# RG-LRU stage in a written TensorE order with its own PSUM, and the later adaLN sums moved to other stages

## The chip, the cores and the metric

The kernel runs on one core of a Trainium2 chip. The metric is device time in microseconds. The core's engines are PE (TensorE), DVE (VectorE), ACT (ScalarE), POOL (GpSimd) and SP (SyncE, which here only issues DMAs); each takes its own instructions in the order in which they stand.

## The reference, cut to what matters

One layer: adaLN modulation, a token mixer with two branches (a bidirectional RG-LRU and a latent attention), their merge, and a mixture of experts. 1024 latent tokens, 256 context tokens, width 1024. What the change touches:

```python
mod = silu(c) @ w_ada + b_ada          # six rows of 1024: shift, scale, gate, twice
z   = modulate(rmsnorm(x)) @ w_in      # RG-LRU input, gelu gate, q/kv latents, sigmoid gates
def rglru_coeffs(x, w_a, b_a, w_x, b_x, lam):
    r = jax.nn.sigmoid(block_diag_linear(x, w_a, b_a))
    i = jax.nn.sigmoid(block_diag_linear(x, w_x, b_x))
    log_a = -RG_C * r * jax.nn.softplus(-lam)
    a = jnp.exp(log_a)
    return a, jnp.sqrt(-jnp.expm1(2.0 * log_a)) * (i * x)
# h = scan(a, b) in both directions over a width-4 convolution of z; y_rnn = (gelu(z') * h) @ w_rnn_out
```

The first two rows of `mod` (shift and scale of the first norm) are needed before anything else. The other four, called m = 0 to 3 in the kernel, are needed from the merge of the branches on.

## The kernel before, in words

Every large matmul is made in three passes (lines 97 to 99, `mm3`): an operand is split by `split` into a high part (an ACT cast, line 93, names ending in h) and the rest (a DVE subtract, line 94, names ending in l), and high×high, high×low and low×high are summed in PSUM. Weights stream from memory through `fetch`: 512 KB into `wr`, split into `wh` and `wl` of three buffers each. A list `items` says in which order; `nextw` takes the next and fetches `LOOK` items ahead.

Where nothing else is said, a scheduler sets the order of instructions on each engine; `tc.manual_schedule` keeps the named engines in the order of the code. Four stages follow one another around the change.

1. q/k/v stage: `qkv` for each of ten token tiles, with blocks of the gelu and sigmoid gates in between (`fill_block`). TensorE's `tp`, `kv`, `zq` and `z` belong to it.
2. RG-LRU stage: eight blocks b of 128 channels. `conv_part(b+1)` projects (48 matmuls `z0` of 512 columns, 24 `z0c` of 256 for the context) and convolves with one ACT and three DVE operations (`xr`, lines 589 and 592). `lru_part(b)` makes four gates (two directions, r and i), each six matmuls `gz` of 512 columns and three `gc` of 256, read by two ACT sigmoids (lines 610 and 611), then tanh, exp, sqrt and DVE scans. `sig_block` makes a sigmoid block `zg` (48 matmuls of 512 columns) of the merge gates; there are 12 in the stage, one to three behind each block b by `sig_plan`. The PSUM comes from two helpers: `pa` (three buffers of two banks: z0, gz, zg, mp) and `pb` (two buffers of one bank: z0c, gc). ACT alone is in written order here.
3. RNN output: for each of eight blocks b of output channels, 96 matmuls `ro` (k = 0 to 7, two halves, three passes) over `rh`/`rl`, the split rows of the RG-LRU's result, then on DVE `s<-ro` (line 821): ro times the sigmoid block, loaded from memory and stored back. Head 0's attention is prepared meanwhile (`qkt`, `pm`, DVE row maxima `mx`, `kl`, `ql`).
4. Attention itself (`s`, and so on).

The adaLN rows m are made by 32 calls of `mod_step`, eight (k) for each m: a 512 KB load of `w_ada` on SP's queue, and on DVE `acc += w_ada[k] * c[k]` (line 395, `acc` 128×1024, one buffer). The eighth call sums `acc` over partitions on TensorE (`mp`, a matmul with ones, line 401), copies the row out on ACT (line 402) and stores it to `mod_d`. A new m begins with a POOL memset of `acc`. All 32 calls stand behind the first eight sigmoid blocks of stage 2, four behind each:

```python
sig_block((s0_d, s1_d)[w][bb], rest if n == 0 else load_rn if b == KD - 1 else None)
for _ in range(4):
    if steps:
        mod_step(steps.pop(0))
```

The router's bias `lb` is made from m = 1 and 2 at the head of stage 3 (`mrow2`, `mc`, `lb`, lines 708 to 720).

Of the kernel before, what the change touches and what calls it, by code (L numbers as in the profile page):

```python
# [24 lines left out]
OP = mybir.AluOpType  # L25
# [35 lines left out]
def layer_kernel(ctx: ExitStack, tc: tile.TileContext, I, rope_tab, out, dbg=None):  # L61
# [324 lines left out]
    def mod_step(j):  # L386
        m, k = divmod(j, KD)
# [18 lines left out]
    with pool("p2") as p2:  # L406
# [151 lines left out]
        for j, i in enumerate(order):  # L558
# [3 lines left out]
            for _ in range(MP2):  # L562
                if steps and steps[0] < N2:
                    mod_step(steps.pop(0))


    p3c = pool("p3")
    p3 = p3c.__enter__()
    if True:
        p4c = None  # L570

        def sig_block(dst, mid=None):
            zz = pa("zg")
            zblock(zz)
# [9 lines left out]
        def conv_part(b):  # L584
            zc, zz = pb("z0c"), pa("z0")
# [12 lines left out]
        def lru_part(b, xr, xrh, xrl):  # L598
            gh, gl_ = nextw([2, 2, P])
            gates = []  # L600
            for d in range(2):
                for g, bn in ((0, "ba"), (1, "bx")):
                    gc, gz = pb("gc"), pa("gz")
# [4 lines left out]
                    r = p3.tile([P, TOK], F32, name=("r", "i")[g], bufs=2)  # L608
# [18 lines left out]
            def rest():  # L627
# [33 lines left out]
        with tc.manual_schedule(engines={mybir.EngineType.Activation}):  # L661
# [21 lines left out]
            for b in range(KD):  # L683
# [24 lines left out]
    mrow = p4.tile([16, P], F32, name="mrow2")  # L708
    nc.sync.dma_start(mrow, mod_d[1:3, :].rearrange("m (k p) -> (m k) p", p=P))
    mc_p = pb("mc")  # L710
    nc.tensor.transpose(mc_p[:, 0:16], mrow, ident[0:16, 0:16])
    mc = p4.tile([P, 2, KD], F32, name="mc")
# [99 lines left out]
    for b in range(KD):  # L812
# [454 lines left out]
```

## Time and profile before

| what | value |
|---|---|
| three runs, median (lowest to highest) | 1790.53 us (1787.06 to 1790.93) |
| the profiled execution's own time | 1793.63 us |
| its span in the trace | 1791.9 us |
| mean granted TensorE clock | 0.976 of full |
| q/k/v stage, about 100.0 to 270.2 | 170.2 us, TensorE busy 168.3 |
| RG-LRU stage, 270.2 to 593.9 | 323.7 us, TensorE busy 309.8 |
| RNN output, 593.9 to 695.7 | 101.8 us, TensorE busy 99.6 |

The span is the time from the first to the last recorded instruction; 1.7 us of the run lie around it. Times of rows are from the span's start. A matmul's row gives a modelled length; neighbours overlap, so its cost is the distance to the next start.

### The profile page before, as it was taken

The numbers are of one execution on the slowest core, as the hardware profiler recorded it, in microseconds if no ns is written. First come the engines' busy times: TensorE is split into PE (matmuls) and PEld (weight loads), VectorE is DVE, ScalarE is ACT, GpSimd is POOL, SyncE is SP. The second block draws the span as 40 slices with busy tenths as digits, with TensorE's granted clock in tenths as the row PEclk, the third lists the DMA queues.
The fourth block names the chain that finished last, engine by engine and source line by source line (L and its number), as shares of the span: only waits on it lengthen the run. The fifth ranks groups of instructions, "written<-read, shape, count | busy, mean of one in ns | idle before, by whom it ended". The sixth has DMA issues, their size and how long they took to land.

```text
span 1791.9 us, 21732 instructions
## 1 busy us (share of the span) xinstructions
PE 1687.7 (94%) x7769; PEld 1346.8 (75%) x7769; DVE 1354.7 (76%) x1852; ACT 1029.6 (57%) x1311; POOL 236.3 (13%) x188
## 2 busy tenths in 40 slices
PE   8999999999899999999999899909999999999997
PEld 3788888787677877777677688708888887888875
DVE  4755445898787554787886857578999999999996
ACT  2532325665677313667776533207777777777774
POOL 1123331111121100111110100000100010001000
PEclk8999999999999999999999999959999999999999
DMA  8264444445452854000000457468999999999971
GB/s 324 98 178 105 112 103 115 133 143 178 134 160 94 280 174 161 28 28 28 28 1 0 180 214 254 187 246 311 384 369 395 390 380 379 389 394 371 390 258 24
DMA packets 177291, 363.80 MB, mean 203 GB/s; under 512 B 43264, under 2 KB 93848, under 8 KB 177184
## 3 DMA queue, kind: packets, MB, share of 16 engines
q1 hardware_dynamic: 172576, 345.65, 53.6%
q0 software_dynamic: 4608, 16.78, 4.1%
q8 instruction: 61, 1.00, 0.2%
q14 instruction: 46, 0.38, 0.1%
HBM read 314.84 MB, written 47.54 MB: 202 GB/s over the span
## 4 chain that ended last, share of the span: by engine, by line
PE 67%; DVE 15%; ACT 6%; issue 6%; DMA 3%; POOL 3%; SPq 0%; POOLq 0%; DVEq 0%; ACTq 0%
PE w_e_gate L98 3%; PE w_e_up L98 3%; PE w_e_gate L97 3%; PE w_e_gate L99 3%; PE w_e_down L98 3%; PE w_e_up L99 3%; PE w_e_up L97 3%; PE w_e_down L99 3%; PE w_e_down L97 3%; PE pm L782 2%; PE z L98 2%; PE z L99 2%; POOL st L142 2%; PE z L97 2%; PE xo L97 2%
## 5 line engine op out<-in xcount | busy, mean ns | idle before, releaser
L94 DVE TENSOR_TENSOR wl<-ma,wh 128x1024 fp32r<-128x1024 f32 x198 | 236.1, 1220 | 21.7 <-ACT wh L93 16.4
L93 ACT CAST wh<-ma 128x1024 fp32r<-128x1024 f32 x198 | 206.7, 1053 | 57.1 <-PE w_e_down L99 18.4
L94 DVE TENSOR_TENSOR wl<-me,wh 128x1024 fp32r<-128x1024 f32 x142 | 170.1, 1221 | 21.6 <-ACT wh L93 16.6
L93 ACT CAST wh<-wr 128x1024 fp32r<-128x1024 f32 (+1 forms) x97 | 98.2, 1014 | 138.9 <-PE z L98 54.6
L93 ACT CAST wh<-me 128x1024 fp32r<-128x1024 f32 x142 | 148.5, 1053 | 47.1 <-PE w_e_down L99 15.6
L846 ACT ACTIVATE pr<-s 128x512 f32<-128x512 f32 x160 | 95.6, 599 | 74.1 <-PE s L99 72.7
L784 DVE TENSOR_REDUCE mx<-pm 128x1 f32<-128x320 f32 x256 | 114.3, 483 | 24.6 <-PE pm L782 21.6
L94 DVE TENSOR_TENSOR wl<-wr,wh 128x1024 fp32r<-128x1024 f32 (+1 forms) x97 | 114.0, 1183 | 24.0 <-ACT wh L93 22.4
L98 PE MATMUL z<-xl,wh 128*128 128x512 f32 x320 | 126.1, 394 | 1.7 <-DVE xl L279 1.7
L99 PE MATMUL z<-xh,wl 128*128 128x512 f32 x320 | 125.7, 394 | 0.6 <-POOL wl L325 0.6
L97 PE MATMUL z<-xh,wh 128*128 128x512 f32 x320 | 125.7, 395 | 0.0
L94 DVE TENSOR_TENSOR pl<-pr,ph 128x1024 fp32r<-128x1024 f32 x64 | 81.3, 1270 | 31.8 <-ACT ph L93 25.0
L98 PE MATMUL w_e_up<-wl,xgh 128*128 128x512 f32 x256 | 103.1, 403 | 1.1 <-DVE wl L94 0.9
L98 PE MATMUL w_e_gate<-wl,xgh 128*128 128x512 f32 x256 | 102.7, 401 | 0.0
L97 PE MATMUL w_e_gate<-wh,xgh 128*128 128x512 f32 x256 | 102.5, 400 | 0.0
L98 PE MATMUL w_e_down<-wl,hdh 128*128 128x512 f32 x256 | 101.6, 397 | 0.6
L1213 POOL DMA_INDIRECT out_dram<-y,icol x16 | 36.3, 2267 | 494.7 <-DVE y L1212 494.7
L99 PE MATMUL w_e_down<-wh,hdl 128*128 128x512 f32 x256 | 99.9, 390 | 0.8 <-DVE hdl L94 0.8
L99 PE MATMUL w_e_gate<-wh,xgl 128*128 128x512 f32 x256 | 100.6, 393 | 0.0
L97 PE MATMUL w_e_down<-wh,hdh 128*128 128x512 f32 x256 | 99.9, 390 | 0.2 <-ACT hdh L93 0.2
L97 PE MATMUL w_e_up<-wh,xgh 128*128 128x512 f32 x256 | 100.1, 391 | 0.0
L99 PE MATMUL w_e_up<-wh,xgl 128*128 128x512 f32 x256 | 100.0, 391 | 0.0
(335 smaller groups left out, 4366.5 us busy)
## 6 DMA issues: line engine op xcount, KB each, us to landing
ma<-in_w_e_down_dram SPq DMA_DIRECT2D x68, 512.0 KB, 8.6
ma<-in_w_e_gate_dram SPq DMA_DIRECT2D x66, 512.0 KB, 7.6
ma<-in_w_e_up_dram SPq DMA_DIRECT2D x64, 512.0 KB, 6.4
me<-in_w_e_gate_dram SPq DMA_DIRECT2D x48, 512.0 KB, 6.4
me<-in_w_e_up_dram SPq DMA_DIRECT2D x48, 512.0 KB, 7.1
me<-in_w_e_down_dram SPq DMA_DIRECT2D x46, 512.0 KB, 8.2
wr<-in_w_in_dram SPq DMA_DIRECT2D x32, 512.0 KB, 4.9
wr<-in_w_ada_dram SPq DMA_DIRECT2D x32, 512.0 KB, 3.4
```

The lines of the kernel that those rows point to most:

```text
L93: nc.scalar.copy(h, src)
L94: nc.vector.tensor_tensor(l, src, h.bitcast(F32), OP.subtract)
L97: nc.tensor.matmul(o, lh, rh, start=start, stop=False)
L98: nc.tensor.matmul(o, lh, rl, start=False, stop=False)
L99: nc.tensor.matmul(o, ll, rh, start=False, stop=stop)
L142: nc.gpsimd.tensor_tensor(ap, ap, h, OP.pow)
L782: nc.tensor.matmul(pm[:, 0:320], qh[:, t * P:(t + 1) * P], kh[:, g * 320:(g + 1) * 320], start=True, stop=True)
L784: nc.vector.tensor_reduce(mx[:, g, t:t + 1], pm[:, 0:320], axis=AX.X, op=OP.max)
L846: nc.scalar.activation(pr[:, sl], sp_, AF.Exp)
L1213: nc.gpsimd.indirect_dma_start(out=out_rows, out_offset=bass.IndirectOffsetOnAxis(ap=icol[:, e:e + 1], axis=0), in_=y, in_offset=None, com ...
```

## The change

- The RG-LRU stage gets a PSUM pool of its own: two buffers of two banks shared by z0 and zg (`pz`), one buffer each for gz (two banks), gc and z0c (one bank).
- PE joins ACT in `manual_schedule`. Each of a block's four gates is followed by an eighth (six matmuls) of the block's first sigmoid block (generator `sig_mm`); its other half comes behind the fourth gate. The tanh moves up behind each direction's gates; r gets a third buffer.
- The 32 sums leave the stage. The eight of m = 1 go to the q/k/v stage, one behind each of eight tiles; the other 24 (m = 2, 0, 3) go into the RNN output, four behind each of the blocks b = 0 to 5. The row is written into `acc[0:1]` instead of a tile of its own.
- The RNN output begins with k = 0 to 6 of block 0, k = 0 to 6 of block 1, then k = 7 of both. The last RG-LRU result is stored on GpSimd's queue.
- `mrow2`, `mc`, `lb` move from the head of the RNN output to its end.

```diff
-    steps = list(range(4 * KD))
+    steps = [(m, k) for m in (1, 2, 0, 3) for k in range(KD)]
+    mod_psum = [pa]
...
-            row = mpool().tile([1, D], F32, name="g", tag="sg", bufs=1)
-            mp = pa("mp")
+            row = acc[0:1, :]
+            mp = mod_psum[0]("mp")
...
-            for _ in range(MP2):
-                if steps and steps[0] < N2:
-                    mod_step(steps.pop(0))
+            mod_steps(1, (1,))
+    open_psum("ps3")
+    def pz(name):
+        return ps["p"].tile([P, 1024], F32, name=name, tag="z", bufs=2)
...
+        def sig_mm(look=None):
+            zz = pz("zg")
+            h, l = nextw([KD, P], look)
+            for n in range(2):
+                for k in range(0, KD, 2):
+                    zhalf(zz, h, l, n, (k, k + 1))
+                    yield zz
...
         def lru_part(b, xr, xrh, xrl):
             gh, gl_ = nextw([2, 2, P])
-            gates = []
+            gates, vv = [], []
+            zg = sig_mm(1)
             for d in range(2):
                 for g, bn in ((0, "ba"), (1, "bx")):
-                    gc, gz = pb("gc"), pa("gz")
+                    gc = ps["p"].tile([P, 512], F32, name="gc", bufs=1)
+                    gz = ps["p"].tile([P, 1024], F32, name="gz", bufs=1)
...
                     mm3(gc[:, 0:CTX], gh[:, g, d], gl_[:, g, d], xrh[:, 0:CTX], xrl[:, 0:CTX], True, True)
-                    r = p3.tile([P, TOK], F32, name=("r", "i")[g], bufs=2)
+                    next(zg)
+                    r = p3.tile([P, TOK], F32, name=("r", "i")[g], bufs=3 - g)
...
-        with tc.manual_schedule(engines={mybir.EngineType.Activation}):
+        with tc.manual_schedule(engines={mybir.EngineType.Activation, mybir.EngineType.PE}):
...
-                    sig_block((s0_d, s1_d)[w][bb], rest if n == 0 else load_rn if b == KD - 1 else None)
-                    for _ in range(4):
-                        if steps:
-                            mod_step(steps.pop(0))
+                    sig_block((s0_d, s1_d)[w][bb], rest if n == 0 else load_rn if b == KD - 1 else None,
+                              zg if n == 0 else None)
...
+    early = []
+    for b in range(2):
+        early.append((pa("ro"), *nextw([KD, P])))
+        ro_mm(*early[b], range(KD - 1))
+    for b in range(KD):
+        if b < 2:
+            po, h, l = early[b]
+            ro_mm(po, h, l, [KD - 1])
+        else:
+            h, l = nextw([KD, P])
+            po = pa("ro")
+            ro_mm(po, h, l, range(KD))
         sg = p4.tile([P, SEQ], F32, name="s0", bufs=1)
         nc.sync.dma_start(sg, s0_d[b])
         nc.vector.tensor_tensor(sg, po, sg, OP.mult)
         nc.sync.dma_start(s0_d[b], sg)
+        mod_steps(4, (2, 0, 3))
```

PE, in the gates of an RG-LRU block, before: gate follows gate without anything between them.

```order
L97 MATMUL gz<-xrh,wh 128x512
L98 MATMUL gz<-xrl,wh 128x512
L99 MATMUL gz<-xrh,wl 128x512
L97 MATMUL gc<-xrh,wh 128x256
L98 MATMUL gc<-xrl,wh 128x256
L99 MATMUL gc<-xrh,wl 128x256
L97 MATMUL gz<-xrh,wh 128x512
```

PE, the same place, after: six matmuls of zg (three are shown) stand between two gates.

```order
L97 MATMUL gc<-xrh,wh 128x256
L98 MATMUL gc<-xrl,wh 128x256
L99 MATMUL gc<-xrh,wl 128x256
L97 MATMUL zg<-xh,wh 128x512
L98 MATMUL zg<-xl,wh 128x512
L99 MATMUL zg<-xh,wl 128x512
...
L97 MATMUL gz<-xrh,wh 128x512
L98 MATMUL gz<-xrl,wh 128x512
```

The gate's tiles have one buffer each now, and the zg between them is the cover. PE, in the RNN output between blocks 0/1 and block 2, after: the rows follow the last `ro` of block 1.

```order
L99 MATMUL ro<-rh_4547,wl 128x512
L783 MATMUL qkt<-ident,kraw 97x128 x4
L783 MATMUL qkt<-ident,qraw 97x128 x4
L783 MATMUL qkt<-ident,kraw 97x128 x4
L796 MATMUL pm<-kh,qh 128x320
L783 MATMUL qkt<-ident,kraw 97x128 x2
L796 MATMUL pm<-kh,qh 128x320
L412 MATMUL mp<-acc,ones 1x512 x2
L97 MATMUL ro<-rh_4444,wh 128x512
```

The sum `mp` of m = 2 stands ahead of all 96 matmuls of block 2; before, no `mp` was in this stage. The sums of m = 0 and m = 3 stand likewise behind blocks 3 and 5, with three and five `pm` ahead of them. DVE, from the product of block 0 to that of block 1, before:

```order
L821 TENSOR_TENSOR s_4757<-ro,s_4757 128x1024
L94 TENSOR_TENSOR wl<-wr,wh 128x1024 x2
L94 TENSOR_TENSOR kl<-qkt,kh 97x512
L94 TENSOR_TENSOR wl<-wr,wh 128x1024
L821 TENSOR_TENSOR s_4816<-ro,s_4816 128x1024
```

DVE, the same place, after:

```order
L848 TENSOR_TENSOR s_4695<-ro,s_4695 128x1024
L94 TENSOR_TENSOR wl<-wr,wh 128x1024
L406 SCALAR_TENSOR_TENSOR acc<-wr,sc,acc 128x1024
L94 TENSOR_TENSOR kl<-qkt,kh 97x512
L406 SCALAR_TENSOR_TENSOR acc<-wr,sc,acc 128x1024
L94 TENSOR_TENSOR ql<-qkt,qh 97x512
L406 SCALAR_TENSOR_TENSOR acc<-wr,sc,acc 128x1024
L94 TENSOR_TENSOR kl<-qkt,kh 97x512
L406 SCALAR_TENSOR_TENSOR acc<-wr,sc,acc 128x1024
L798 TENSOR_REDUCE mx<-pm 128x1
L406 SCALAR_TENSOR_TENSOR acc<-wr,sc,acc 128x1024
L848 TENSOR_TENSOR s_4720<-ro,s_4720 128x1024
```

Three of the eight `acc` of m = 2 stand ahead of these rows, the last five stand among them, behind `s<-ro` of block 0.

## Rows read from the trace of the kernel before

**Rows 1.** The page's part 1: busy time, share and instructions of each engine.
```profile
PE 1687.7 (94%) x7769; PEld 1346.8 (75%) x7769; DVE 1354.7 (76%) x1852; ACT 1029.6 (57%) x1311; POOL 236.3 (13%) x188
```

**Rows 2.** Windows, three stages: window, length, busy PE PEld DVE ACT POOL; clock, DMA share, GB/s.
```profile
100.00:270.20 170.20, 168.34 (x828) 147.05 (x827) 86.96 (x268) 48.81 (x105) 55.87 (x49) 1.00 0.47 115
270.20:593.90 323.70, 309.75 (x1446) 250.80 (x1444) 261.05 (x226) 203.83 (x208) 55.53 (x22) 0.99 0.44 138
593.90:695.70 101.80, 99.59 (x459) 81.16 (x459) 45.79 (x71) 21.73 (x26) 5.08 (x8) 0.98 0.61 211
```

**Rows 3.** What TensorE waited for in the RG-LRU stage: total us, times, longest.
```profile
PE gc L97 <- DVE xr L592: 10.1, 6, 3.6
PE gz L97 <- ACT r L610: 3.8, 6, 0.6
```

**Rows 4.** Groups of TensorE in the RG-LRU stage: busy us, mean ns | idle.
```profile
L97 PE MATMUL zg<-xh,wh 128*128 128x512 f32 x192 | 75.4, 393 | 0.0
```

**Rows 5.** Timeline of TensorE at the RG-LRU stage's end: start, length.
```profile
592.27 0.39 PE L97 MATMUL zg<-xh,wh 128*128 128x512 f32 x1
...
593.40 0.39 PE L99 MATMUL zg<-xh,wl 128*128 128x512 f32 x1
```

**Rows 6.** Timeline of one RG-LRU block's first gates.
```profile
487.86 0.28 PE L99 MATMUL z0c<-xh,wl 128*128 128x256 f32 x1
...
487.98 0.40 PE L97 MATMUL gz<-xrh,wh 128*128 128x512 f32 x1
...
488.70 1.20 ACT L589 ACTIVATE xr<-z,colv 128x1024 f32<-128x1024 f32 x1
...
490.73 1.12 ACT L610 ACTIVATE r<-gz,colv 128x1024 f32<-128x1024 f32 x1
...
491.90 0.50 PE L97 MATMUL gz<-xrh,wh 128*128 128x512 f32 x1 [0.64 <-ACT r L610]
```

**Rows 7.** The chain, around 350 us: start, length, what.
```profile
350.62 1.81 PE mp L401 x4
```

**Rows 8.** Groups of VectorE in the RG-LRU stage: the adaLN sums.
```profile
L395 DVE SCALAR_TENSOR_TENSOR acc<-wr,sc,acc 128x1024 f32<-128x1024 f32 x32 | 48.6, 1519 | 12.9 <-DMA wr<-in_w_ada_dram 12.7
```

**Rows 9.** Timeline of TensorE, last tile of the q/k/v stage.
```profile
267.03 0.27 PE L474 MATMUL tp<-ident,zn 128*128 128x128 f32 x1
...
268.74 0.50 PE L97 MATMUL kv<-ukv,zh 128*128 128x512 f32 x1
```

**Rows 10.** Timeline of VectorE, start of the RNN output.
```profile
599.08 2.36 DVE L94 TENSOR_TENSOR rl<-wr,rh 128x1024 fp32r<-128x1024 f32 x2
...
607.47 2.57 DVE L94 TENSOR_TENSOR rl<-wr,rh 128x1024 fp32r<-128x1024 f32 x2 [0.94 <-ACT rh L93]
614.37 1.22 DVE L821 TENSOR_TENSOR s<-ro,s 128x1024 f32<-128x1024 f32 x1 [4.33 <-PE ro L99]
615.51 1.22 DVE L94 TENSOR_TENSOR wl<-wr,wh 128x1024 fp32r<-128x1024 f32 x1
```

**Rows 11.** Timeline, the longest wait of TensorE in the RNN output.
```profile
644.60 1.22 DVE L821 TENSOR_TENSOR s<-ro,s 128x1024 f32<-128x1024 f32 x1 [6.98 <-DMA s<-s_d]
645.74 0.88 DVE L784 TENSOR_REDUCE mx<-pm 128x1 f32<-128x320 f32 x2
...
646.37 0.52 PE L782 MATMUL pm<-kh,qh 97*128 97x320 f32 x1 [2.04 <-DVE mx L784]
```

**Rows 12.** Groups of VectorE in the RNN output: row maxima.
```profile
L784 DVE TENSOR_REDUCE mx<-pm 128x1 f32<-128x320 f32 x32 | 14.5, 486 | 3.5 <-PE pm L782 2.4
```

**Rows 13.** The line that loads the adaLN weights: landing of its transfers.
```profile
DMA to landing us min/median/max: 3.3/3.4/5.0
```

**Rows 14.** Timeline of TensorE behind the RNN output's last block.
```profile
697.20 0.50 PE L97 MATMUL s<-qh,kh 97*128 97x512 f32 x1 [0.62 <-DVE s L821]
```

**Rows 15.** Windows behind two waits of TensorE (columns as in Rows 2).
```profile
456.50:462.30 5.80, 5.80 (x17) 4.85 (x18) 4.72 (x4) 2.69 (x4) 0.67 (x1) 0.51 0.44 119
...
646.40:649.80 3.40, 3.40 (x10) 2.84 (x11) 2.64 (x5) 0.00 (x0) 0.00 (x0) 0.51 0.44 164
```

More of the change, by code (lines that the diff above doesn't have):

```diff
@@ L336, in nextw, with look_ahead @@
         return ahead[n]
+    def look_ahead():
+        n = taken[0]
+        taken[0] = n - 1 + LOOK
+        fetch()
+        taken[0] = n
     LOOK = 2
     NFIRST = 3
-    MP2, N2 = 1, 0
     def zhalf(dst, h, l, n, ks=range(KD)):
@@ L384, in layer_kernel, with mod_steps, mod_step @@
     macc = {}
-    def mod_step(j):
-        m, k = divmod(j, KD)
+    def mod_steps(n, m1):
+        for _ in range(n):
+            if steps and steps[0][0] in m1:
+                mod_step(*steps.pop(0))
+    def mod_step(m, k):
         if k == 0:
@@ L570, in layer_kernel, with sig_block @@
         p4c = None
-        def sig_block(dst, mid=None):
-            zz = pa("zg")
-            zblock(zz)
+        def sig_mm(look=None):
[5 more added lines that the diff above has]
+                    yield zz
+        def sig_block(dst, mid=None, mm=None):
+            for zz in mm or sig_mm():
+                pass
             if mid:
@@ L584, in conv_part @@
         def conv_part(b):
-            zc, zz = pb("z0c"), pa("z0")
+            zc, zz = ps["p"].tile([P, 512], F32, name="z0c", bufs=1), pz("z0")
             zblock(zz, zc[:, 0:CTX])
@@ L617, in lru_part @@
                 vv.append(v)
+            look_ahead()
+            av = []
             for d in range(2):
@@ L707, in layer_kernel @@
     nc.sync.dma_start(wr, krows(I["w_router"][0], 0, NE))
[L708 to L712, printed above, removed]
-    nc.vector.tensor_copy(mc, mc_p[:, 0:16].rearrange("p (m k) -> p m k", m=2))
-    nc.vector.scalar_tensor_tensor(mc[:, 1], mc[:, 1], 1.0, col("g2", 0, 8), op0=OP.add, op1=OP.mult)
-    lb_p = pb("lb")
-    for k in range(KD):
-        nc.tensor.matmul(lb_p[:, 0:NE], mc[:, 0, k:k + 1].to_broadcast([P, P]), wr[:, k, :], start=(k == 0), stop=(k == KD - 1))
-    lb = consts.tile([P, NE], F32, name="lb")
-    nc.vector.tensor_copy(lb, lb_p[:, 0:NE])
-    nc.vector.tensor_tensor(wr, wr, mc[:, 1, :, None].to_broadcast([P, KD, NE]), OP.mult)
     p5c = pool("p5", side="right")
@@ L811, in layer_kernel, with ro_mm @@
     pre = [f for fs in head_ops(0) for f in fs]
-    for b in range(KD):
-        h, l = nextw([KD, P])
-        po = pa("ro")
-        for k in range(KD):
+    def ro_mm(po, h, l, ks):
+        for k in ks:
             for n in range(2):
@@ L825, in layer_kernel @@
                 pre.pop(0)()
+    assert not steps
+    mrow = p4.tile([16, P], F32, name="mrow2")
+    nc.sync.dma_start(mrow, mod_d[1:3, :].rearrange("m (k p) -> (m k) p", p=P))
+    mc_p = pb("mc")
+    nc.tensor.transpose(mc_p[:, 0:16], mrow, ident[0:16, 0:16])
+    mc = p4.tile([P, 2, KD], F32, name="mc")
+    nc.vector.tensor_copy(mc, mc_p[:, 0:16].rearrange("p (m k) -> p m k", m=2))
+    nc.vector.scalar_tensor_tensor(mc[:, 1], mc[:, 1], 1.0, col("g2", 0, 8), op0=OP.add, op1=OP.mult)
+    lb_p = pb("lb")
+    for k in range(KD):
+        nc.tensor.matmul(lb_p[:, 0:NE], mc[:, 0, k:k + 1].to_broadcast([P, P]), wr[:, k, :], start=(k == 0), stop=(k == KD - 1))
+    lb = consts.tile([P, NE], F32, name="lb")
+    nc.vector.tensor_copy(lb, lb_p[:, 0:NE])
+    nc.vector.tensor_tensor(wr, wr, mc[:, 1, :, None].to_broadcast([P, KD, NE]), OP.mult)
     p4c.__exit__(None, None, None)
```

16 lines of the change are left out of this document (8 added, 8 removed).

## The prediction

> **What bounds the kernel now.** I read the page's busy shares first: TensorE is busy 94% of the span, VectorE 76% [rows 1]. The share says little of the stages, so next come the windows of the three that the change touches. TensorE works nearly all of each; what differs is VectorE's part: 87 of 170 us in the q/k/v stage, 261 of 324 in the RG-LRU stage, 46 of 102 in the RNN output [rows 2]. The third view is TensorE's waits in the RG-LRU stage: 10.1 us in which `gc` waits for the convolution's `xr` and 3.8 in which `gz` waits for a sigmoid [rows 3]. The first is a buffer, not data: gc and z0c share the two buffers of `pb`, and z0c's is free only once line 592 has read it. These two are the 13.9 us of that stage in which TensorE is idle.
>
> **The RG-LRU stage.** Counted by the code it has 1152 matmuls of 512 columns (192 of each pass for zg alone [rows 4], 128 for z0, 64 for gz) and 288 of 256. At the stage's end five steps from 592.27 to 593.40 give 0.226 us for one of 512 [rows 5], and 487.86 to 487.98 gives 0.12 for one of 256 [rows 6]. That is 260.4 + 34.6 = 295.0. The four sums `mp` are 1.81 each on the path [rows 7], 7.2 in all. The stage takes 323.7, and 13 z0c (1.6 us) were done ahead of it; so 325.3 - 302.2 = 23 us are lost, which I round to 22.5 since other stretches step at 0.227. Of it 13.9 are the waits and some 9 matmuls that step more slowly around them.
>
> After the change z0c and gc have banks of their own, so the 10.1 goes. The price is the single gz buffer. In one block of before, gz starts at 487.98, directly behind z0c; ACT is then still at the convolution's copy (488.70, 1.20 us) and a weight cast, and the sigmoid runs from 490.73 until the next gz gets its buffer at 491.90 [rows 6]: 3.9 us from the first matmul to a free buffer. ACT's order ahead of the first sigmoid is unchanged. The new PE order has gz 6 × 0.226, gc 3 × 0.12 and an eighth of zg 6 × 0.226 in that time, 3.1 us. So each block's first gate leaves a wait of 0.8 us, with the restart some 1.25 (0.8 to 2). Later gates are covered: a gate's two sigmoids, 1.6 us, fit into the 3.1. Seven blocks have a convolution ahead: 8.8 us. The stage gains 22.5 - 8.8 + 7.2 = 20.9. Bounds: if the slow 9 stay, 13.9 - 8.8 + 7.2 = 12; if no wait is left, 29.7. VectorE loses 48.6 us of work here [rows 8], which frees it but is off TensorE's path; I give it nothing more.
>
> A rule speaks against the single buffer. The Trainium skill, Trainium Kernel Development and Optimization, in Best Practices, says to double-buffer for performance, of DMA beside compute. Carried over to a PSUM tile it would leave each of 32 gates exposed to its two sigmoids, and by that the stage would lose what the order gains (the second rival below). The row says that only the first gate of a block is exposed, since the work between two gates is longer than the sigmoids.
>
> **The q/k/v stage.** One sum of 1.81 comes in. The last tile's `tp` at 267.03 was followed by 13 z0c, and `kv` started at 268.74 [rows 9]: 1.7 us in which the normalisation ran beside them. PE in written order keeps z0c in the next stage, so kv stands directly behind tp: 1.7 more. Eight `acc` go to a VectorE that is half idle; 0.5 for delays. Sum 4.0 (2 to 6).
>
> **The RNN output**, in the order in which TensorE meets it:
>
> - Three sums at 1.81: 5.4.
> - The start. In written order k = 2 to 6 of block 0 are wanted in steps of 6 × 0.226 = 1.36 us, from 2.7 us after the stage's begin (593.9) to 8.2. In the trace the last `rl` are made from 599.08 to 610.0 [rows 10], 5 to 16 us behind it, the last of them k = 7, which now comes after k = 6 of block 1. For k = 6 I take 13 us. Before, the scheduler filled this with matmuls of two blocks in any order; now block 0 waits some 5 us (0 to 7).
> - The sum of m = 2 stands ahead of block 2. Its last `acc` stands on VectorE behind `s<-ro` of block 0, a `wl`, four `acc`, three small subtracts and a row maximum. From block 0's end: 1.22 + 1.22 [rows 10], five acc at 1.28 (the mean of 32 in the RG-LRU stage is 1.52 [rows 8], where POOL and ACT are busy too; for this quieter stage I estimate 1.28, near the 1.22 of a subtract of the same size), three subtracts at 0.6 (half of 1.22, they have 512 columns), 0.49 for the maximum [rows 12]: 11.1 us. TensorE has k = 7 of block 1, 1.36, and qkt and pm of about 1.5 to do. Wait: 8.2. If VectorE took ready work first, only the load would bind: s stored (1.22), two loads of 3.4 behind it [rows 13] and an acc, 6.6, less 2.9: 3.7. With acc at 1.52: 9.4.
> - The sum of m = 0 stands behind block 3 and three pm; on VectorE s of block 3, acc, mx, acc: 1.22 + 1.28 + 0.49 + 1.28 = 4.3, less 0.7: 3.6 (2 to 5).
> - The sum of m = 3: s of block 5 and one acc, 2.5, and ahead of them three acc between the maxima on which pm waits, 3.8: together 6 (0 to 7).
> - The end: lb now follows block 7: VectorE does s, mc, a wl, mc again, 1.22 + 0.2 + 1.22 + 0.2 = 2.8, then TensorE goes on: 3 (1.5 to 4).
> - The clock. Behind before's 3.57 us wait the granted clock was 0.51 for 5.8 us, the lower of its levels of 1.2 and 2.4 GHz: 2.9 lost. Behind a 2.04 us wait it was 3.4 us: 1.7 lost [rows 15]. Two new waits of such length: 5.8 (2.9 to 11.6).
> - What before loses itself goes: the 2.04 behind mx [rows 11], its 1.7 of clock, and the 0.62 at the end [rows 14]; with a small one 4.5.
>
> Sum: 5.4 + 5 + 8.2 + 3.6 + 6 + 3 + 5.8 - 4.5 = 32.5 (11 to 45, with low or high values throughout).
>
> That a queue holds ready work behind work that isn't is in the trace: s at 644.60 waited 6.98 us for a transfer, mx came behind it at 645.74, and TensorE's pm had to wait 2.04 for that [rows 11]. The Trainium skill, PSUM — Partial Sum Buffer, section Engine vs sequencer instructions, calls the queues of ScalarE, VectorE and GpSimdE strict FIFO, and the trace agrees. By that rule the wait for m = 2 is 8.2; without it 3.7, and the forecast some 4.5 lower.
>
> **Sum.** -20.9 + 4.0 + 32.5 = +15.6. The profiled execution took 1793.6 us, 3.1 over the median of the three; its waits stand in both. 1793.6 + 15.6 = 1809.2, or from the median 1790.5 + 15.6 = 1806.
>
> **Rivals.**
> - *The sums are ready when TensorE gets to them* (faster). The three waits, 17.8, and their clock, 5.8, fall out of the RNN output: 32.5 - 23.6 = 8.9, net -8.0, 1782.5. For it: VectorE has 56 idle us in that stage and 24 acc need 31. Against it: five acc are behind s of block 0 by order, with 2.9 us of TensorE's work for cover. It decides below 20.9 - 4.0 = 16.9 us lost in the RNN output.
> - *The RG-LRU stage doesn't get shorter by more than its sums.* If ACT's order lets the single gz set the pace, the waits grow to what goes: gain 7.2, net -7.2 + 4.0 + 32.5 = +29.3, 1820. For it: gz waits 3.8 us for the sigmoid with three buffers already [rows 3]. Against: 3.1 us of cover that it lacked.
> - *A draw.* Only the wait for m = 2 with its clock holds, and the start is covered: 5.4 + 8.2 + 3 + 2.9 - 4.5 = 15.0, net -1.9, 1789.
>
> **How the numbers follow.** Forecast 0.60, sums ready 0.20, no gain in the RG-LRU stage 0.11, draw 0.09. Under about 0.2% (3.6 us) this kernel's measurement can't tell from no change, so the draw is "same"; some of the forecast's low tail goes to it and to faster: faster 0.22, same 0.10, slower 0.68. The range reaches from the faster rival, 1781, to the third, 1819.
>
> **What would show it.** RG-LRU stage at 303 us (294 to 312) with gc waits gone and seven gz waits of about 1 us. RNN output at 134 us (113 to 147), TensorE waiting for VectorE's acc ahead of mp, the longest behind blocks 0 and 1, with clock at 0.5 behind it. If the stage stays below 119, the forecast is wrong and the sums were hidden; if the RG-LRU stage is above 312, the single gz is the reason.

## The result, and the profile after

The changed kernel takes 1820.3 us (median of 4 runs, 1815.81 to 1822.41) against 1788.8 for the kernel before (4 runs): ratio 1.0179, 95% interval 1.0161 to 1.0198, 31.5 us more. The forecast was 1806 and at most 1819: right in sign, half in size. The profiled execution took 1822.41 us, 28.8 more than that of before. (A block of the RNN output has 48 matmuls `ro`, 8 k × 2 halves × 3 passes, not 96 as the description of the kernel says; no term of the sum used that number.)

Windows of the changed kernel, the three stages of [rows 2] (columns as there):

```profile
100.00:279.20 179.20, 170.89 (x816) 145.91 (x815) 95.65 (x275) 48.87 (x105) 60.63 (x49) 0.99 0.51 130
279.20:585.80 306.60, 300.66 (x1442) 251.34 (x1441) 231.65 (x193) 199.92 (x204) 51.02 (x19) 0.99 0.28 89
585.80:724.00 138.20, 116.35 (x473) 84.44 (x471) 77.09 (x95) 27.13 (x30) 7.67 (x10) 0.91 0.74 254
```

The q/k/v stage ends 10.5 us later (279.2; before 270.2, less the 1.6 us of z0c done ahead, 268.7), the RG-LRU stage is 18.6 shorter (306.6 against 325.2), the RNN output 36.4 longer (138.2 against 101.8). That is 28.3 of the 28.8 us. In the last stage TensorE's busy time grew by 16.8 us, of which the three sums are 5.4 at full clock. The other 11.4 are for the most part clock: 0.91 on average over 138.2 us is 12.4 us lost, against 2.0 at 0.98 over 101.8 before.

TensorE's waits of the changed kernel, in this order: q/k/v (two lines), RG-LRU (one line, for [rows 3]), RNN output (seven lines):

```profile
PE kv L99 <- DVE zl L94: 6.8, 5, 2.0
PE kv L97 <- ACT zh L93: 1.4, 1, 1.4
...
PE gz L97 <- ACT r L638: 5.8, 7, 2.0
...
PE pm L796 <- DVE mx L798: 5.5, 4, 4.1
PE ro L97 <- ACT rh L93: 4.5, 2, 3.7
PE mp L412 <- DVE acc L406: 4.3, 3, 3.0
PE qkt L783 <- DVE kl L94: 3.2, 2, 2.0
PE ro L98 <- DVE rl L94: 1.9, 3, 0.8
PE lb L864 <- DVE mc L860: 1.3, 1, 1.3
PE pm L796 <- DVE ql L94: 1.1, 1, 1.1
```

The gc waits of [rows 3] are gone, and gz waits 5.8 us (8.8 forecast). In the RNN output TensorE waits for VectorE in 17.3 of the 21.8 us; the other 4.5 are the casts of rh at the start. The timeline of VectorE from block 0's product (compare [rows 10]) to the last acc of m = 2, and TensorE's mp:

```profile
615.56 1.22 DVE L848 TENSOR_TENSOR s<-ro,s 128x1024 f32<-128x1024 f32 x1 [0.28 <-PE ro L99]
616.70 1.22 DVE L94 TENSOR_TENSOR wl<-wr,wh 128x1024 fp32r<-128x1024 f32 x1
617.83 1.28 DVE L406 SCALAR_TENSOR_TENSOR acc<-wr,sc,acc 128x1024 f32<-128x1024 f32 x1
...
624.41 0.49 DVE L798 TENSOR_REDUCE mx<-pm 128x1 f32<-128x320 f32 x1
624.81 1.28 DVE L406 SCALAR_TENSOR_TENSOR acc<-wr,sc,acc 128x1024 f32<-128x1024 f32 x1
...
626.14 3.57 PE L412 MATMUL mp<-acc,ones 128*1 128x512 f32 x4 [0.56 <-DVE acc L406]
```

From 615.56 to 626.09 are 10.5 us; the forecast had counted 11.1 in this order, with 1.28 for an acc. TensorE waited less than forecast in one piece, since qkt and pm stood ahead of mp and waited themselves for kl, ql and mx of the same queue: 5.7 us in all. From 616.70 to 626.10, behind block 1, TensorE was busy for 3.8 us, where the forecast had 1.5 for qkt and pm; the granted clock of these 9.4 us was 0.69. And mp took 3.57 us instead of 1.81 [rows 7]: TensorE was at the lower clock (0.50 from 626.10 to 629.70). Windows of that stretch:

```profile
606.00:626.00 20.00, 14.47 (x65) 11.09 (x63) 15.52 (x15) 4.86 (x7) 1.97 (x3) 0.86 0.95 318
626.00:641.00 15.00, 14.86 (x52) 9.78 (x53) 4.55 (x6) 2.04 (x2) 0.95 (x1) 0.85 0.84 285
```

In the second TensorE hardly waits and has a mean clock of 0.85: some 2 us paid after the waits, most of them in mp itself.

### The profile page after: what moved, and what is told of

Same layout as the page of the kernel before. It is cut to its first block, busy times and chain, and to the rows that moved or that the text cites. A ratio compares the mean times of both kernels' runs of the same rounds, so it can differ in the third digit from the quotient of the medians.

```text
span 1820.6 us, 21747 instructions
## 1 busy us (share of the span) xinstructions
PE 1700.6 (93%) x7769; PEld 1353.8 (74%) x7769; DVE 1363.9 (75%) x1852; ACT 1029.6 (57%) x1311; POOL 239.7 (13%) x189
## 4 chain that ended last, share of the span: by engine, by line
PE 71%; DVE 11%; issue 6%; ACT 5%; POOL 3%; DMA 3%; SPq 0%; POOLq 0%; ACTq 0%; DVEq 0%
PE w_e_gate L98 3%; PE w_e_up L98 3%; PE w_e_gate L97 3%; PE w_e_gate L99 3%; PE w_e_down L98 3%; PE w_e_up L99 3%; PE w_e_up L97 3%; PE w_e_down L99 3%; PE w_e_down L97 3%; PE z L98 2%; PE z L97 2%; PE z L99 2%; POOL st L142 2%; PE pm L796 2%; PE s L97 2%
## 5 line engine op out<-in xcount | busy, mean ns | idle before, releaser
L93 ACT CAST wh<-ma 128x1024 fp32r<-128x1024 f32 x198 | 206.6, 1052 | 57.5 <-PE w_e_down L99 18.6
L94 DVE TENSOR_TENSOR wl<-wr,wh 128x1024 fp32r<-128x1024 f32 (+1 forms) x97 | 129.4, 1341 | 67.6 <-ACT wh L93 66.3
L94 DVE TENSOR_TENSOR pl<-pr,ph 128x1024 fp32r<-128x1024 f32 x64 | 81.0, 1266 | 31.5 <-ACT ph L93 24.7
L97 PE MATMUL w_e_up<-wh,xgh 128*128 128x512 f32 x256 | 100.2, 391 | 0.0
L99 PE MATMUL w_e_up<-wh,xgl 128*128 128x512 f32 x256 | 100.2, 391 | 0.0
```

The source lines that it names most:

```text
L93: nc.scalar.copy(h, src)
L94: nc.vector.tensor_tensor(l, src, h.bitcast(F32), OP.subtract)
L97: nc.tensor.matmul(o, lh, rh, start=start, stop=False)
L99: nc.tensor.matmul(o, ll, rh, start=False, stop=stop)
```

## The experiments

Stages of all runs, measured in their traces as above (the RG-LRU stage up to the first ro, the RNN output up to the first s of the attention; where 13 z0c were done ahead, their 1.6 us are counted to the RG-LRU stage). Each ratio is to runs of before made beside that kernel, with medians of 1788.8 to 1791.7 us; the stages come from one trace of each kernel:

| run | time | ratio to before | q/k/v end | RG-LRU | RNN output |
|---|---|---|---|---|---|
| before | 1790 | 1 | 268.7 | 325.2 | 101.8 |
| changed | 1820.3 | 1.0179 (1.0161 to 1.0198) | 279.2 | 306.6 | 138.2 |
| moves_alone | 1819.8 | 1.0166 (1.0140 to 1.0192) | 278.3 | 305.4 | 139.5 |
| sums_late | 1804.3 | 1.0080 (1.0057 to 1.0103) | 282.4 | 306.6 | 117.2 |
| late_and_any_order | 1798.3 | 1.0047 (1.0028 to 1.0065) | 279.0 | 305.0 | 116.3 |
| blocks_interleaved | 1800.7 | 1.0059 (1.0040 to 1.0078) | 280.1 | 305.0 | 116.2 |
| qkv_without_acc | 1814.3 | 1.0134 (1.0103 to 1.0165) | 272.1 | 306.4 | 137.3 |
| qkv_free | 1825.7 | 1.0205 (1.0180 to 1.0229) | 272.1 | 321.5 | 135.0 |
| qkv_free_2 | 1841.6 | 1.0276 (1.0241 to 1.0311) | 273.3 | 332.9 | 133.9 |
| sums_back | 1836.9 | 1.0267 (1.0244 to 1.0290) | 270.5 | 361.5 | 102.6 |
| gates_only | 1834.3 | 1.0230 (1.0209 to 1.0251) | 273.1 | 361.1 | 102.1 |
| gates_only_2 | 1832.2 | 1.0237 (1.0204 to 1.0270) | 272.7 | 359.7 | 101.2 |
| mp_in_gz_2r | 1802.8 | 1.0065 (1.0044 to 1.0086) | 270.1 | 334.6 | 101.0 |
| mp_in_gz_3r | 1902.9 | 1.0628 (1.0609 to 1.0647) | 270.6 | 434.7 | 102.9 |
| two_r | 1832.1 | 1.0219 (1.0190 to 1.0249) | 279.1 | 313.8 | 144.2 |
| sums_on_gpsimd | 1868.8 | 1.0422 (1.0400 to 1.0443) | 272.8 | 396.8 | 103.5 |
| eight_in_stage | 1801.5 | 1.0061 (1.0045 to 1.0078) | 272.1 | 317.2 | 115.2 |
| own_banks | 1790.8 | 1.0006 (0.9996 to 1.0016) | 271.3 | 320.7 | 101.4 |
| fixed_banks | 1786.1 | 0.9974 (0.9960 to 0.9988) | 271.6 | 315.7 | 100.2 |

The q/k/v end scatters: without acc in that stage it lies from 268.7 to 273.3, with them from 278.3 to 282.4. The profiled run of before is the lowest.

**Where the moved sums cost.** First, the moves without the order and the PSUM:

```diff
# moves_alone, on the kernel before
+    steps = [(m, k) for m in (1, 2, 0, 3) for k in range(KD)]
+            mod_steps(1, (1,))                 # q/k/v
-                    for _ in range(4):         # RG-LRU stage
-                        if steps:
-                            mod_step(steps.pop(0))
+        mod_steps(4, (2, 0, 3))                # RNN output; mrow2, mc, lb at its end
```

> The kernel before with the sums moved as in the change (eight in q/k/v, 24 in the RNN output, router bias at the end), and nothing else: gates, PSUM and the order of the first two RNN output blocks as before. Theory: the moved sums cost by VectorE's order. RG-LRU stage 318 (7.2 less) or somewhat under, q/k/v 8 to 10 longer, RNN output 28 to 36 longer: 1788.8 - 8 + 9 + 31 = 1821. Rival: the written order (RG-LRU stage, first two blocks) makes most of the loss in the RNN output. Then RNN output is at most 12 longer and the time about 1802.

The time came as the first theory said, and q/k/v with it (9.6 longer); the RNN output was 37.7 longer, just over its 28 to 36. The RG-LRU stage was 12.6 shorter than the theory had it, so the time was met by luck in part. It took 305.4 us, as short as with the written order and the own PSUM. Its waits (compare [rows 3]):

```profile
PE gc L97 <- ACT r L613: 4.0, 4, 1.0
PE gc L97 <- DVE xr L594: 1.8, 3, 0.9
PE gz L97 <- ACT r L612: 1.0, 1, 1.0
```

The 10.1 us of gc on xr are 1.8 here, with the shared banks still in place: VectorE, without 48.6 us of sums, reads z0c in time. So in the change the order and the banks bring nothing measurable on top.

The trace of before has this already, at the longest of its six waits of gc on xr:

```profile
447.21 0.56 ACT L589 ACTIVATE xr<-z0c,colv 128x256 f32<-128x256 f32 x1 [7.61 <-PE z0c L99]
...
450.25 2.60 DVE L395 SCALAR_TENSOR_TENSOR acc<-wr,sc,acc 128x1024 f32<-128x1024 f32 x2 [8.84 <-DMA wr<-in_w_ada_dram]
...
455.94 0.47 DVE L592 SCALAR_TENSOR_TENSOR xr<-z0c,colv,xr 128x255 f32<-128x255 f32 x1
...
456.47 0.58 PE L97 MATMUL gc<-xrh,wh 128*128 128x256 f32 x1 [3.57 <-DVE xr L592]
```

ACT had read z0c by 447.8. VectorE stood at two sums until their load landed, then did the convolution behind them, and gc started when the last read of z0c was done. At the other five waits, too, a sum stands right ahead of the xr rows or among them. A rival is that the row of a sum shared the sigmoid's buffer in before, so that ACT waited 19.6 us for it in the stage (four times 4 to 6 us), and the moves end that too. None of TensorE's twelve waits there ends at that copy.

Next, the changed kernel with each mp one block later:

```diff
# sums_late
-            mp = mod_psum[0]("mp")             # at k == 7; matmul, copy and store go to mod_sum
+            sums.append((m, acc))
+        mod_sum()                              # ahead of the next block's steps
         mod_steps(4, (2, 0, 3))
-            macc[m] = mpool().tile([P, D], F32, name="acc", bufs=1)
+            macc[m] = mpool().tile([P, D], F32, name="acc", bufs=1 if m == 1 else 2)
```

> The changed kernel with each sum over partitions in the RNN output put one block later (the sum of m = 2 behind block 2 instead of block 1, of m = 0 behind block 4, of m = 3 behind block 6; acc has two buffers there), all else as it is. Theory: TensorE stands at mp because the last acc is behind s<-ro of the block just done; a block later it is long done. The waits at and around the three sums (14 us) and their low clock (some 8) go: RNN output from 138 to 118, 1801. Rival: VectorE has too much to do at once (24 acc between maxima and products) and TensorE waits for pm's maxima instead. Then RNN output stays over 130 and the time over 1813.

RNN output 117.2, as forecast; VectorE has as much to do (77.7 us), so it isn't short of time. The waits that are left:

```profile
PE ro L97 <- ACT rh L93: 4.0, 2, 3.7
PE qkt L791 <- DVE kl L94: 1.6, 1, 1.6
PE ro L98 <- DVE rl L94: 1.5, 2, 0.8
PE lb L874 <- DVE mc L870: 1.3, 1, 1.3
```

Two attempts on the start. `late_and_any_order` puts the plain loop over b back; `blocks_interleaved` writes k by k:

```diff
# late_and_any_order, on sums_late
-        ro_mm(*early[b], range(KD - 1))
+    for b in range(KD):
+        ro_mm(po, h, l, range(KD))
# blocks_interleaved, on sums_late
+    for k in range(KD):
+        for b in range(2):
+            ro_mm(*early[b], [k])
```

> The kernel with the sums one block later in the RNN output (117.2 us there, 1804), and also the first two blocks of the RNN output written as a plain loop as before, so that the scheduler orders them. Theory: the written order (k = 0 to 6 of both, then k = 7) makes TensorE wait for rh and rl at the start, 5.5 us and 3 of low clock. RNN output 108 to 110, time 1796. Rival: the start waits for data that no order has earlier. Then 115 to 118 and 1803.

> The kernel with the sums one block later in the RNN output (117.2 us there, 1804), with the first two blocks of that stage written k by k in turn (k = 0 of block 0, of block 1, k = 1 of block 0, ...). The kernel before has such an order there and no wait; both later kernels go through seven or eight k of block 0 first and wait 5.5 to 7 us for rh and rl. Theory: each k then has 2.7 us of matmuls instead of 1.4, and the rows arrive in 2.7 to 3 us steps; the wait falls to 2 or less, with its clock some 3: RNN output 111 to 113, time 1799. Rival: the rows come later than that: 116 to 118, time 1803 or more.

Neither shortened the stage (116.3 and 116.2). With the plain loop the scheduler still put all of block 0 first, so the order hardly changed: the test says little. With k by k the waits for rh and rl went, and one of 6.3 us came:

```profile
PE ro L97 <- ACT wr L614: 6.3, 1, 6.3
```

That is a sigmoid (line 614) which must be read before ro gets its bank in the new PSUM pool. So at the start the rows and the bank come about equally late; which of the two the change's order pays for is not settled. The time of the first, 1798.3, is nearer its theory than the stage is, since its q/k/v end came earlier by the scatter. In moves_alone, where the scheduler mixed the blocks as before, TensorE waited 1.6 us at the start instead of 6.4, and yet the stage was no shorter (139.5).

For q/k/v, the eight additions of m = 1 left out (that row then lacks its sum):

```diff
# qkv_without_acc
-        nc.vector.scalar_tensor_tensor(acc, raw, sc[:, k, 0:1], acc, op0=OP.mult, op1=OP.add)
+        if m != 1:
+            nc.vector.scalar_tensor_tensor(acc, raw, sc[:, k, 0:1], acc, op0=OP.mult, op1=OP.add)
```

> The changed kernel without the eight VectorE additions of m = 1 in the q/k/v stage (that row of the adaLN output then lacks its sum; the loads, the mp matmul and the copy stay). Theory: q/k/v is 10.5 us longer than before because acc stands on VectorE ahead of zl and zn; then the stage's end comes at 273 to 275 instead of 279.2, the waits of kv for zl fall from 6.8 to about 2, and the time is 1815. Rival: the loads on SP's queue, the mp and the written order make it; then 277 or later, and 1819 or more.

End at 272.1 (279.2), kv's waits for zl 3.4 (6.8), time 6 us less. The additions are 10.2 us of VectorE in that stage of the changed kernel and cost 7.1 of TensorE's (one trace against one; the scatter of the end is 4 to 5 us, and the means of the runs with and without them differ by 8):

```profile
L406 DVE SCALAR_TENSOR_TENSOR acc<-wr,sc,acc 128x1024 f32<-128x1024 f32 x8 | 10.2, 1280 | 2.0 <-DMA wr<-in_w_ada_dram 2.0
```

How they cost it is only in part their place in VectorE's queue. Of the five waits of kv for zl one, the first, has a sum right ahead of the splits wl and zl. Four of the eight sums ran beside GpSimd's small operation `st` of the norm, which then took 0.97 us longer, and VectorE's next operation waits for it. The first three rows are from the changed kernel, the last from the run without additions:

```profile
168.83 1.28 DVE L406 SCALAR_TENSOR_TENSOR acc<-wr,sc,acc 128x1024 f32<-128x1024 f32 x1
169.00 2.60 POOL L142 TENSOR_TENSOR st<-st,eps 128x8 f32<-128x8 f32 x1 [1.86 <-DVE st L498]
171.64 0.69 DVE L503 TENSOR_TENSOR kf<-kv,st 128x512 f32<-128x512 f32 x1 [1.52 <-POOL st L142]
...
164.32 1.63 POOL L142 TENSOR_TENSOR st<-st,eps 128x8 f32<-128x8 f32 x1 [1.86 <-DVE st L499]
```

These four are 3.9 us of GpSimd's time; how the 7.1 divide between the two ways is not shown.

Two runs put these eight back into the RG-LRU stage of the changed kernel, mp in a buffer of z0 and zg: `qkv_free` (sigmoid output through a weight buffer) and `qkv_free_2` (own buffer, r in two).

```diff
-            mod_steps(1, (1,))                 # q/k/v
+        mod_psum[0] = pz
+                    if n == 0:
+                        mod_steps(1, (1,))     # ahead of sig_block; mod_sum() behind it
```

> The changed kernel with the eight sums of m = 1 back in the RG-LRU stage (one in front of each block's first sigmoid block, the sum over partitions behind block 7's first) instead of in q/k/v. Theory: in q/k/v each sum stands on VectorE ahead of zl, on which TensorE's kv waits (8.3 us of waits against 1.9 before), plus the sum and its clock. q/k/v goes from 10.5 over before to about 2 (the lost cover between tp and kv), RG-LRU stage 2 to 3 longer: 6 us faster than the changed kernel, 1814. Rival: q/k/v lost its time by TensorE's written order, which took z0c out of the last tile and changed the scheduler's choices. Then q/k/v stays 8 or more over before, and the time is 1821.

> As the earlier test with the sums of m = 1 back in the RG-LRU stage, but with the sigmoid blocks in their own buffer and r with two. q/k/v stage as there, 272 to 273 at its end. If eight sums cost the RG-LRU stage little beyond the 1.8 us of the one mp, it takes 308 to 312 (there 321.5) and the time is 1816. If each sum there costs what it did before (18.6 us for 32, so 4.6 for 8, or more), the stage is 311 to 316 and the time 1820, as the changed kernel.

q/k/v came back to 272 to 273 in both, as the theory said, but the RG-LRU stage grew by 15 and 26 us, so neither time was met. What those buffers cost is next.

**What the written order is worth with the sums in the stage.** Four runs have order and PSUM of the change, all 32 sums in the stage, and the RNN output and lb as before:

```diff
# gates_only_2 (gates_only: mod_steps ahead of sig_block; sums_back: also sg in a "wr" buffer, r as in the change)
+        mod_psum[0] = pz
+                    mod_steps(4, range(4))     # behind sig_block
-                    r = p3.tile([P, TOK], F32, name=("r", "i")[g], bufs=3 - g)
+                    r = p3.tile([P, TOK], F32, name=("r", "i")[g], bufs=2)
# mp_in_gz_2r, on gates_only_2
-        mod_psum[0] = pz
+        mod_psum[0] = lambda name: ps["p"].tile([P, 1024], F32, name=name, tag="gz", bufs=1)
```

> The RG-LRU stage of the change, with all 32 adaLN sums back in it (four in front of each of the first eight sigmoid blocks, the sum over partitions behind the block, in the stage's own PSUM; the sigmoid's output goes through a weight buffer to make room), the router bias at the head and the RNN output without the two first blocks' written order, both as before. Theory: the gates' order and PSUM gain by themselves, and the loss comes from where the sums went. The RG-LRU stage then takes the 306.5 us of the changed kernel plus 7 for the four sums, 314 to 319 (before 325), q/k/v and RNN output stand within 3 us of before: 8 us faster than before, 1780. Rival: the stage only got shorter since VectorE lost 48 us of sums. Then it goes back to about 325, and the time to 1790.

> As the first test with all 32 sums back in the RG-LRU stage, but without its fault: sigmoid blocks go to their own buffer as before (there they took a weight buffer, and the weights and TensorE waited 39 us); r has two buffers to make room. So: gates' written order and own PSUM alone, sums in the stage. First theory (the buffers of z0c and gc were the 10 us wait): stage 306.6 + 7.2 + a little = 314 to 318, time 1781. Second theory, which the run with the sums moved alone spoke for (stage 305.4 with the gates as before): the stage gained only because VectorE lost 48 us of sums. Then it is 322 to 328 here, and the time 1790 to 1794.

> As the run with the gates' order alone and all sums in the RG-LRU stage (361 us there), with the sums put behind each sigmoid block as before instead of in front of it. The matmul order on TensorE is the same in both; on SP's queue the gate weights of one block come ahead of four adaLN loads instead of behind them. If the earlier run's loss is that placing (ScalarE once waited 15 us for gate weights), the stage takes about 325 here and the time is near 1794. If the written order itself doesn't bear the sums (weights late, ScalarE's order held by a cast), it stays over 340 and the time over 1812.

All three take about 360 us, some 35 over before, which only the rival of the last had. I first blamed the weight buffer and then the placing; neither changed the time much. In gates_only each long wait of TensorE but the last, at the change of pools, stands behind an mp. ACT and TensorE there:

```profile
362.53 1.02 ACT L612 ACTIVATE sg<-zg 128x1024 f32<-128x1024 f32 x1
363.45 0.98 ACT L420 COPY acc<-mp 1x1024 f32<-1x1024 f32 x1
...
363.61 0.79 PE L97 MATMUL z<-xh,wh 128*128 128x512 f32 x1 [6.75 <-ACT sg L612]
```

mp holds one of the two buffers of z0 and zg, and the other is full until ACT, in its written order, comes to the sigmoid. Four such waits are 26.7 us. The rest are 10.3 of gz on the sigmoids and 7.4 at the change of pools.

> The run with the gates' order alone and the sums behind each sigmoid block (359.7 us in the RG-LRU stage), with mp in the gates' gz buffer, which is free between blocks, instead of one of the two of z0 and zg. Theory: the four waits of 6.4 to 6.8 us behind mp (26.7 us) and their clock go; what is left is the 10.3 us of gz waits, with r in two buffers: 322 to 330, time 1790 to 1798, so the order gains nothing with the sums in the stage. Rival: late weights hold ScalarE whatever mp does; then 345 or more and 1815 or more.

> As the run before this one (mp in the gz buffer), but with three buffers for r and the sigmoid's output through a weight buffer to make room. If r's third buffer matters, gz waits fall from 10 to about 6 us and the stage is 5 shorter than with two, 316 to 324, time 1783 to 1791, the best that this order could give with all sums in the stage. If the weight buffer costs more than that, it is 330 or more and 1798 or more.

> The changed kernel with two buffers for r instead of three, nothing else (no sums in the stage). If r's third buffer is what the gate order needs, the RG-LRU stage goes from 306.6 to 312 or more and the time to 1826 or more; if it isn't, 305 to 308 and 1819 to 1822.

With mp in gz's buffer the four waits go (334.6 us, 4.6 over what I expected), and these stay:

```profile
PE gz L97 <- ACT r L637: 12.7, 8, 2.7
PE ro L97 <- ACT wr L605: 7.0, 1, 7.0
```

Two buffers for r cost the changed kernel 7.2 us in that stage (two_r, 313.8), so the change needs the third one; another 6.0 in its RNN output, where it waits 9.0 us for rh instead of 4.5, I can't explain. With acc in the stage, room for the third was made by sending the sigmoid through a weight buffer, and that failed: mp_in_gz_3r takes 434.7 us, with 86 us of waits ahead of mp. The view names no engine for them, but its rows show what ended them. The first of the four:

```profile
366.44 1.02 ACT L605 ACTIVATE wr<-zg 128x1024 f32<-128x1024 f32 x1
367.49 0.33 SPq L606 DMA_DIRECT2D s_d<-wr  x1
367.92 4.96 SPq L405 DMA_DIRECT2D wr<-in_w_ada_dram  x2
...
379.35 1.27 DVE L406 SCALAR_TENSOR_TENSOR acc<-wr,sc,acc 128x1024 f32<-128x1024 f32 x1
...
380.72 1.01 PE L412 MATMUL mp<-acc,ones 128*1 128x512 f32 x1 [21.40 <-issue]
```

All four mp start 0.1 us behind the end of their last sum on VectorE. The last two loads for these sums went out only behind the store of the sigmoid, which now sits in one of the four weight buffers and which ACT makes late in its written order; meanwhile TensorE, in written order too, stands at mp with no work of its own. In these runs the written order gains nowhere with the sums in the stage.

**The shared bank.** The prediction said that gc waits for a bank which z0c holds. Two kernels test it on the kernel before, sums and order as they were:

```diff
# own_banks
+    open_psum("ps3")                           # and open_psum("ps4") behind the stage
-            zc, zz = pb("z0c"), pa("z0")
+            zc, zz = pz("z0c"), pa("z0")       # pz: one bank for each name
# fixed_banks
     def pb(name="pb"):
-        return ps["p"].tile([P, 512], F32, name=name, tag="b", bufs=2)
+        turn[0] += 1
+        one = {"gc": 0, "z0c": 1}.get(name, turn[0] % 2)
+        return ps["p"].tile([P, 512], F32, name=name, tag=f"b{one}", bufs=1)
```

> The kernel before with one edit: in the RG-LRU stage z0c and gc have one bank each of their own instead of two shared ones; order, sums and all else as before. The prediction's step: gc's 10.1 us of waits for xr of line 592 are a shared buffer, so they go, the stage takes 312 to 316 (before 325) and the time is 1780. Second theory: the waits come from VectorE being late with the sums in its queue; then TensorE waits for the same lateness elsewhere (z0c or gc for their single buffer, gz), the stage stays at 321 to 327 and the time at 1787 to 1793.

> The kernel before with one edit and no change of pools: the two single PSUM banks of pb are told apart, gc always takes the one and z0c the other, all else takes them in turn. Sums, order and stages as before. If gc's 10.1 us of waits are a bank that z0c still holds, and nothing else is late behind it, the RG-LRU stage takes 312 to 316 (before 325), q/k/v and RNN output are as before, and the time is 1777 to 1781, the best of all. If VectorE's lateness comes out at another wait, the stage stays over 320 and the time over 1785.

Waits of TensorE in the RG-LRU stage of own_banks:

```profile
PE ro L97 <- ACT wr L586: 5.7, 1, 5.7
PE gz L97 <- ACT r L615: 3.8, 6, 0.6
PE z0c L97 <- DVE xr L597: 1.8, 1, 1.8
PE zg L97 <- DVE xr L597: 1.4, 1, 1.4
```

and of fixed_banks:

```profile
PE gz L101 <- ACT r L614: 3.8, 6, 0.6
PE zg L101 <- DVE xr L596: 2.2, 1, 2.2
PE z0c L101 <- DVE xr L596: 1.4, 1, 1.4
```

gc's 10.1 us are gone in both; 3.2 and 3.6 come out elsewhere. own_banks gave the gain back at the change of pools (5.7 us at the first ro, and 1.4 in which kv waits behind tp). fixed_banks, without that change, has a stage of 315.7 us, as expected, and is the one kernel faster than before: ratio 0.9974 (0.9960 to 0.9988), 4 us. The time, 1786.1, is 5 us over what I expected; its q/k/v end is 2.9 later than in the trace of before, which is within the scatter of that stage.

**Other homes for the sums.**

```diff
# sums_on_gpsimd, on the kernel before
-        nc.vector.scalar_tensor_tensor(acc, raw, sc[:, k, 0:1], acc, op0=OP.mult, op1=OP.add)
+        nc.gpsimd.tensor_scalar(raw, raw, sc[:, k, 0:1], None, op0=OP.mult)
+        nc.gpsimd.tensor_tensor(acc, acc, raw, OP.add)
# eight_in_stage, on moves_alone with the later mp: m = 1 here instead of in q/k/v
+                    if n == 0:
+                        mod_steps(1, (1,))
+                    mod_sum()
```

> The kernel before with one edit: the 32 adaLN products and additions are done on GpSimd (a multiply and an add) instead of VectorE, in the same place. If VectorE's queue is what the sums cost the RG-LRU stage, it takes 305.4 + 7.2 for the four mp = 313 (before 325), and the time is 1778. Rival: GpSimd's own product i*xr (16 of 3.1 us) comes behind sums of some 5 us each, and the scans behind it, and VectorE is slowed beside GpSimd. Then the stage stays at 323 or more, and the time at 1789 or over.

> The kernel before (gates, PSUM and the two first RNN output blocks as before) with the sums of m = 1 in the RG-LRU stage, one behind each block's first sigmoid block, the other 24 in the RNN output with the sum over partitions one block later, and the router bias at the end. What the runs so far suggest as a better place. If the stage's cost of the sums falls with their number (19.8 us for 32), it takes 309 to 312 with eight; q/k/v as before, 269; RNN output 110 to 117: 1778 to 1788. If the eight cost as much as they did beside the written order (332.9 for that stage), 1800 or more.

GpSimd was worse by far: 396.8 us. A sum takes 3.6 + 2.7 us there (spans of GpSimd are rough in the profile), GpSimd stands 75 us more at the loads of w_ada, and its product for the scans comes behind both. Groups of GpSimd in that stage:

```profile
L395 POOL TENSOR_SCALAR wr<-wr,sc 128x1024 f32<-128x1024 f32 x32 | 116.6, 3646 | 80.2 <-DMA wr<-in_w_ada_dram 75.0 <-DVE r L637 5.2
L396 POOL TENSOR_TENSOR acc<-acc,wr 128x1024 f32<-128x1024 f32 x32 | 87.0, 2719 | 12.1 <-DMA acc<-in_b_ada_dram 9.6
```

and TensorE's longest wait there:

```profile
PE gc L97 <- DVE xr L593: 52.4, 7, 14.3
```

VectorE is slowed beside it as well, as the rival had said. A group of VectorE's in before, and the same here, twice as long:

```profile
L622 DVE TENSOR_TENSOR r<-av 128x1280 f32<-128x1280 f32 x16 | 23.1, 1488 | 33.1 <-ACT av L621 33.1
...
L623 DVE TENSOR_TENSOR r<-av 128x1280 f32<-128x1280 f32 x16 | 46.1, 2919 | 65.9 <-ACT av L622 65.9
```

Eight sums in the stage cost 317.2 - 305.4 = 12 us, not a quarter of 19.8, and the time, 1801.5, is 13 over what I expected: the cost isn't in proportion to their number. Of TensorE's waits there 8.2 us are gc waiting, four times, for a sigmoid of ACT; why ACT is late I did not follow up.

## Why the prediction was right in sign and wrong in size

- *RG-LRU stage: forecast -20.9, measured -18.6.* The size held, but by luck in part: the reason given was not the only one. That gc's wait is a shared bank is right by itself (fixed_banks, 9.5 us), but it needs two things: the bank and a VectorE late with sums. The change removes both, and either alone is enough: moves_alone gives -19.8 without banks or order. "VectorE loses 48.6 us of work here, which frees it but is off TensorE's path; I give it nothing more" was the step that failed here: the sums alone held the convolution back, up to 3.57 us at a time. The waits of the first gates were 5.8 us, 0.83 for each of seven, as the bare 0.8 of the forecast; with the restart it had 8.8.
- *q/k/v stage: forecast +4.0, measured +10.5, some 8 by the mean of the runs.* This is the step that put the time out of the range: "Eight `acc` go to a VectorE that is half idle; 0.5 for delays." They cost 7.1 (qkv_without_acc). What held the work back, the queue, which I priced in the RNN output, and GpSimd's `st` beside the sums, was not priced here; the busy share of 87 of 170 us [rows 2] hid that the chain up to zl has no slack. mp and the lost cover came as forecast (3.5): without the additions the stage ends 3.4 after that of before, 1.8 for mp and 1.4 in which kv waits behind tp. Against the mean of the other runs it is less, within the scatter.
- *RNN output: forecast +32.5, measured +36.4.* The mechanism held: mp stood behind VectorE's queue, and one block later it is 21 us cheaper (sums_late). (The 6.6 us for "ready work first" is not the sum of the parts named for it, 1.22, two loads of 3.4 and an acc, which are 9.3 one behind the other; by these the other reading of m = 2 gives 6.4 and not 3.7.) The waits are 21.9 us (25.8 forecast): start 6.4 (5), m = 2 with the qkt and pm ahead of it 5.7 (8.2), m = 0 4.8 (3.6), m = 3 3.6 (6), lb 1.3 (3). The clock was mis-sized: "Two new waits of such length: 5.8", less 1.7 that before lost itself, is 4.1; the part of TensorE's busy time that the work doesn't explain grew by 11.4 us. Short waits in a row cost clock too (0.86 from 606 to 626), and the sums themselves run at the lower one: the median of the 16 matmuls mp is 1.01 us, against 0.59 before.
- *Rivals.* "The sums are ready" did not come; nor did "no gain in the RG-LRU stage", in which the single gz would have set the pace, nor the draw: the RNN output lost more than twice what it had.

So 13 us of error are 6.5 in q/k/v, 3.9 in the RNN output (clock up, waits down) and 2.3 in the RG-LRU stage. The rest of the 31.5 by medians is the scatter of before.

## What to carry to other kernels

A busy share of a half did not tell here whether an operation could be added: look at what stands behind it in the same queue, what runs beside it on GpSimd, and who waits for these. A sum whose last part was just queued should be asked for a block later, not next. Two causes that make one wait (a shared bank, a late reader) don't add up: take the cheaper one away first and measure, here a few lines instead of a new order and a new pool. They gained 4 us, 0.26%.

## What the runs showed that I had not expected

- A change of PSUM pools is not free: TensorE waited 5.7 to 7.0 us for the last sigmoid at the start of the next stage (own_banks, mp_in_gz_2r). In the changed kernel, which has the change too, no such wait is seen; there the rows were late instead.
- One more tile in a two-buffer pool cost 6.4 to 6.8 us each time, because ACT in written order came late to free the other (gates_only).
- On GpSimd the 128×1024 product with one column took 3.65 us and the addition of two tiles 2.72 (means of 32, beside a busy VectorE), so one input was not faster than two; VectorE does both in one operation of 1.28. VectorE and GpSimd also slowed each other: 2.92 for 1.49 us of an operation on VectorE in that run, 2.60 for 1.63 of a small operation on GpSimd beside a sum.
- The adaLN operation on VectorE took 1.28 us in the quiet stages. In the RG-LRU stage of before its median is 1.28 as well; the mean of 1.52 [rows 8] comes from a few of up to 3.99.
